# A two-layer SSD and pooling trunk step whose instruction order comes from the tile framework's other simulation

## The chip, the cores and the metric

The kernel runs on one core of one Trainium2 chip. Its metric is the device time of one execution, in microseconds (us). The text speaks of five engines: PE (matrix multiply, with PEld for its weight loads), DVE (vector), ACT (scalar, functions by table), POOL (general), and SP, which here only issues transfers.

## The reference

One inference step of a two-layer trunk with model width 1024, over one prompt of 1024 new tokens and eight samples of eight tokens each, so 1088 token columns in all. Cut to what matters:

```python
for i in range(2):
    mod = silu(c) @ ada_w[i] + ada_b[i]
    shift, scale, gate = split(mod, 3)
    hn = rmsnorm(x, norm_g[i]) * (1 + scale) + shift
    if i == 0:      # Mamba-2 SSD: in-projection, causal conv of width 4, chunked scan, gated norm, out-projection
        out, ... = ssd_branch(hn, ...)
    else:           # pooling: u, z = hn @ w_in; causal means over 2, 4, 8, 16 tokens; grouped matmul; * silu(z); @ w_out
        out, ... = pool_branch(hn, ...)
    x = x + gate * out
y = rmsnorm(x, final_norm_g)
```

The scan runs in chunks of 128 tokens over 8 groups of 4 heads. The outputs are y, the new SSM states, and the last rows of the convolution and of the pooling branch.

## The kernel before

Activations lie with the 1024 model rows on 128 partitions times 8 k blocks and the 1088 tokens along the free axis. Every fp32 operand of a large product is split in a rounded high half (`hh`, `wh`, `gh`: ACT, by L319, L139, L174, L742) and the rest as a low half (`hl`, `wl`, `gl`: DVE or POOL, by L320, L140, L176, L743), and each product is three matmuls: high by high, low by high, high by low (L182 to L184, L980 to L982, L1196 to L1198). Wide products go in two ways: plainly, in three column chunks of 364, 364 and 360 tokens, or in pairs by a scheme of seven half-size products instead of eight (`st` tiles, sums of operands in `t`).

In time the stages are these, in us from the start of the span:

- 0 to 75, the front: adaLN vectors (`am`, L253), the first norm, then for each k block the modulation (L316, L322, L323) and at once its matmuls;
- 75 to 350: the first layer's in-projections (`front_pairs`);
- 350 to 925: the scan, group by group. One step of a scan chunk is: transposes `tr` (L545, L549); from them `cb` and `xd` (DVE L559, L562) and `Bt` (ACT L566); masks `M` (ACT L556, L557); decays `cd` (ACT L574) and `ea` (ACT L543), which need `acb`, a row fetched by a transfer through a ring of two buffers; the state product `S` (PE L588); state updates (L596, L597); and `y` (PE L609, L613). Between the steps stand, as filling, further in-projections (their results leave PSUM by ACT L419) and out-projections (`mm`, whose results are gated and added by DVE L764);
- 925 to 1075: the end of the out-projection, the second layer's norm and its plain products `pl`. Here three column chunks are normalised in turn: squares summed over k (`ss`, L781), their sum over partitions (`ms`, PE L293, two matmuls), `rst` (ACT L296, L309), the scaled rows (DVE L316), shift and rounding (ACT L318, L319), and `hl` (DVE L320);
- 1075 to 1360: the fast pairs of the second layer, 1360 to 1470 the pooling and its grouped product;
- 1470 to 1632: the last out-projection, in seven blocks, the last of which is followed quarter by quarter by the final norm: `ms` (L293), `rst` (L296), the scale (L1648, L309), `y` (DVE L1661, POOL L1659) and ten transfers of the result.

The order of the instructions on each engine is not the order of the code. The tile framework's scheduler takes, for each engine, the earliest instruction of the program that its simulation says can run now. The code sets limits to it: buffer counts of the pools (two `acb`, two `wh` and `wl`, three `mm`), `issue_after`, which holds a group of instructions back behind a given one, and `keep_in_program_order`. On the chip each engine then takes its instructions strictly in the order so fixed, and waits where an operand is late.

## Time and profile before

| what | value |
| --- | --- |
| median of 3 runs | 1631.87 us |
| lowest and highest | 1627.06 and 1631.94 us |
| profiled execution, span | 1632.2 us |
| PE busy | 1601.1 us (98%) |
| DVE busy | 1290.3 us (79%) |
| ACT busy | 816.7 us (50%) |
| POOL busy | 495.2 us (30%) |
| mean granted clock of PE | 0.994 |

The profiled execution lies 0.3 us above the median of the runs. The chain of work that ended last runs over PE for 82% of the span, over DVE for 7% and over transfers for 5%. A row of a timeline gives start, busy time, engine, line, operation, tiles and shapes, and in brackets the idle time of the engine before it and what ended that.

### The profile page before, as it was taken

The page shows a single profiled execution, that of the slowest core. Times are in us where ns is not written, and L with a number is a line of the kernel's source. Part 1 is how long each engine was busy: PE and PEld are TensorE (multiplying, and loading weights), DVE is VectorE, ACT ScalarE, POOL GpSimd, SP SyncE. Part 2 cuts the span into 40 slices and gives each one's busy share as a digit, 9 for nine tenths or more (in the row PEclk, how much of TensorE's full clock was granted, in tenths as well). Part 3 has the DMA queues.
Part 4 walks back from the last instruction along what each step waited for, and adds up shares of the span by engine and source line. Part 5 has one row for each costly group of instructions (what it writes and reads, how often), then busy time and mean ns, then how long its engine had stood idle before and what let it go on. Part 6 is the DMA issues. An engine that isn't in the chain of part 4 may idle for free.

```text
span 1632.2 us, 30956 instructions
## 1 busy us (share of the span) xinstructions
PE 1601.1 (98%) x12061; PEld 1524.7 (93%) x12061; DVE 1290.3 (79%) x2140; ACT 816.7 (50%) x1565; POOL 495.2 (30%) x527
## 2 busy tenths in 40 slices
PE   8999999999999999999999999999999999999997
PEld 6899999998899888988998899999999999999997
DVE  6875779777788888789887867988889867577876
ACT  6653334456776767575645536632322333333364
POOL 0233556511221202121212222366667640000241
PEclk9999999999999999999999999999999999999999
DMA  9422232264555554668898533043333369565783
GB/s 346 163 98 84 93 109 71 105 203 133 183 162 167 165 186 135 217 232 299 276 332 284 201 137 111 29 142 112 102 112 99 129 213 367 166 170 173 167 164 119
DMA packets 122306, 275.60 MB, mean 169 GB/s; under 512 B 18192, under 2 KB 59312, under 8 KB 122160
## 3 DMA queue, kind: packets, MB, share of 16 engines
q1 hardware_dynamic: 118128, 260.91, 46.8%
q0 software_dynamic: 4032, 12.72, 4.5%
q8 instruction: 95, 1.56, 0.4%
q14 instruction: 51, 0.42, 0.1%
HBM read 201.12 MB, written 70.23 MB: 166 GB/s over the span
## 4 chain that ended last, share of the span: by engine, by line
PE 82%; DVE 7%; DMA 5%; issue 3%; ACT 2%; POOL 1%; SPq 0%; DVEq 0%; ACTq 0%; POOLq 0%
PE st L982 11%; PE st L980 11%; PE st L981 11%; PE mm L182 10%; PE mm L184 10%; PE mm L183 10%; DMA acb<-acd 2%; PE op L1197 2%; PE op L1198 2%; PE op L1196 2%; PE y L609 2%; PE S L588 2%; PE y L613 2%; PE am L253 1%; PE tr L549 1%
## 5 line engine op out<-in xcount | busy, mean ns | idle before, releaser
L982 PE MATMUL st<-hh,w 128*128 128x272 f32 x832 | 240.8, 289 | 2.3 <-DVE w L176 2.3
L980 PE MATMUL st<-hh,w 128*128 128x272 f32 x832 | 240.2, 289 | 0.0
L981 PE MATMUL st<-hl,w 128*128 128x272 f32 x832 | 239.7, 288 | 0.0
L982 PE MATMUL st<-t,w 128*128 128x272 f32 x624 | 179.6, 288 | 0.0
L980 PE MATMUL st<-t,w 128*128 128x272 f32 x624 | 179.6, 288 | 0.0
L981 PE MATMUL st<-t,w 128*128 128x272 f32 x624 | 179.2, 287 | 0.0
L182 PE MATMUL mm<-hh,wh 128*128 128x364 f32 (+1 forms) x528 | 178.4, 338 | 0.1
L184 PE MATMUL mm<-hh,wl 128*128 128x364 f32 (+1 forms) x528 | 174.6, 331 | 0.0
L183 PE MATMUL mm<-hl,wh 128*128 128x364 f32 (+1 forms) x528 | 173.7, 329 | 0.0
L174 ACT ACTIVATE w<-wr 128x512 fp32r<-128x512 f32 x104 | 65.6, 631 | 190.4 <-PE st L982 156.8
L982 PEld LDWEIGHTS st<-hh,w 128*128 128x128 f32 x832 | 156.4, 188 | 3.4 <-DVE w L176 3.4
L980 PEld LDWEIGHTS st<-hh,w 128*128 128x128 f32 x832 | 156.7, 188 | 0.3 <-issue 0.3
L981 PEld LDWEIGHTS st<-hl,w 128*128 128x128 f32 x832 | 156.8, 188 | 0.0
L596 POOL TENSOR_TENSOR hd<-h,cd 128x256 f32<-128x256 f32 x56 | 47.1, 842 | 353.6 <-DVE h L597 195.4
L182 PE MATMUL mm<-gh,wh 128*128 128x364 f32 (+1 forms) x384 | 130.2, 340 | 2.1 <-ACT raw L419 2.1
L1197 PE MATMUL op<-b,w 128*128 128x272 f32 x448 | 129.0, 288 | 1.3 <-DVE b L1126 1.3
L1198 PE MATMUL op<-b,w 128*128 128x272 f32 x448 | 129.0, 288 | 0.7 <-DVE w L1170 0.7
L1196 PE MATMUL op<-b,w 128*128 128x272 f32 x448 | 129.6, 289 | 0.0
L184 PE MATMUL mm<-gh,wl 128*128 128x364 f32 (+1 forms) x384 | 127.1, 331 | 0.0
L183 PE MATMUL mm<-gl,wh 128*128 128x364 f32 (+1 forms) x384 | 126.7, 330 | 0.1
L980 PEld LDWEIGHTS st<-t,w 128*128 128x128 f32 x624 | 117.7, 189 | 0.0
L982 PEld LDWEIGHTS st<-t,w 128*128 128x128 f32 x624 | 117.3, 188 | 0.0
(293 smaller groups left out, 4613.7 us busy)
## 6 DMA issues: line engine op xcount, KB each, us to landing
wr<-win SPq DMA_DIRECT2D x48, 512.0 KB, 3.7
acb<-acd SPq DMA_DIRECT2D x64, 256.0 KB, 3.9
wr<-pin SPq DMA_DIRECT2D x32, 512.0 KB, 3.6
wr<-pout SPq DMA_DIRECT2D x28, 512.0 KB, 3.9
x<-x1d SPq DMA_DIRECT2D x24, 544.0 KB, 6.3
x1d<-x SPq DMA_DIRECT2D x22, 544.0 KB, 5.4
wr<-pout POOLq DMA_DIRECT2D x20, 512.0 KB, 5.5
x<-xT SPq DMA_DIRECT2D x16, 544.0 KB, 6.0
```

The costliest lines, as they stand in the source:

```text
L174: self.nc.scalar.activation(hi, src, AF.Copy)
L182: nc.tensor.matmul(ps[:, :n], hi[:, k, :], ah[:, a:a + n], start=first, stop=False)
L183: nc.tensor.matmul(ps[:, :n], hi[:, k, :], al[:, a:a + n], start=False, stop=False)
L184: nc.tensor.matmul(ps[:, :n], lo[:, k, :], ah[:, a:a + n], start=False, stop=last)
L588: nc.tensor.matmul(S[:, 256 * i:256 * i + 256], Bt, xde.rearrange("p r q -> p (r q)"), start=True, stop=True)
L596: nc.gpsimd.tensor_tensor(out=hd, in0=h[-1], in1=cd.unsqueeze(2).to_broadcast([P, 4, 64]), op=ALU.mult)
L980: nc.tensor.matmul(ps[c][:, :QUART], hi[:, k], xh[:, t], start=(k == 0), stop=False)
L981: nc.tensor.matmul(ps[c][:, :QUART], hi[:, k], xl[:, t], start=False, stop=False)
L982: nc.tensor.matmul(ps[c][:, :QUART], lo[:, k], xh[:, t], start=False, stop=(k == 3))
L1196: nc.tensor.matmul(ps[:, :QUART], hi[:, k], xh, start=k == 0, stop=False)
L1197: nc.tensor.matmul(ps[:, :QUART], hi[:, k], xl, start=False, stop=False)
L1198: nc.tensor.matmul(ps[:, :QUART], lo[:, k], xh, start=False, stop=k == 7)
```

## The change

One argument is added where the framework's context is made. The scheduler itself stays; the simulation that tells it what can run when is another, a time-line simulation in place of the default one.

```diff
-    with tile.TileContext(nc) as tc:
+    with tile.TileContext(nc, schedule_with_timeline_sim=True) as tc:
```

The instructions are the same, but for two more loads of ACT's function table, where an exponential (L484) now stands between two gate chunks. What changes is the order on each engine: on PE instructions move by up to 99 places, on DVE by up to 39, on ACT by up to 29. In the long runs of `st` matmuls (about 160 to 320 and 1080 to 1360 us) PE's order is unchanged. Three places, first ACT in the scan near 902 us. `Bt_10578` is needed by the second `S` of a step, `cd_10696` needs the transfer into `acb_10612`:

```order
+L139 ACTIVATE wh_10538<-wr_10317 128x1024
+L557 ACTIVATE M_10621<-M_10621 128x512
 L543 ACTIVATE ea_10614<-acb_10558 128x512
-L566 ACTIVATE Bt_10498<-tr_10482 128x128
-L557 ACTIVATE M_10567<-M_10567 128x512
-L556 ACTIVATE M_10621<-acb_10558,tka_1431 128x128 x2
-L139 ACTIVATE wh_10538<-wr_10317 128x1024
-L556 ACTIVATE M_10621<-acb_10558,tka_1431 128x128 x2
+L566 ACTIVATE Bt_10578<-tr_10562 128x128
 L574 ACTIVATE cd_10696<-acb_10612 128x4
-L557 ACTIVATE M_10621<-M_10621 128x512
-L566 ACTIVATE Bt_10578<-tr_10562 128x128
```

`Bt_10578` moves from behind `cd_10696` to ahead of it. Next DVE at the start of the second layer, near 1000 us, in the first column chunk. `hl_11576`, `hl_11578` and so on are the low halves of the eight k blocks, `wl_11825` a weight's low half. Before:

```order
L316 TENSOR_SCALAR x_10311<-x_10311,scl_270,rst_11192 128x364
L316 TENSOR_SCALAR x_10439<-x_10439,scl_270,rst_11192 128x364
L316 TENSOR_SCALAR x_10536<-x_10536,scl_270,rst_11192 128x364
L320 TENSOR_TENSOR hl_11576<-x_10307,hh_11575 128x364
L320 TENSOR_TENSOR hl_11578<-x_10309,hh_11577 128x364
L316 TENSOR_SCALAR x_10699<-x_10699,scl_270,rst_11192 128x364
L320 TENSOR_TENSOR hl_11580<-x_10311,hh_11579 128x364
L320 TENSOR_TENSOR hl_11582<-x_10439,hh_11581 128x364
```

and now:

```order
L316 TENSOR_SCALAR x_10699<-x_10699,scl_270,rst_11192 128x364
L316 TENSOR_SCALAR x_10904<-x_10904,scl_270,rst_11192 128x364
L316 TENSOR_SCALAR x_10975<-x_10975,scl_270,rst_11192 128x364
L769 TENSOR_TENSOR x_10904<-x_10904,gs_11714 128x64
L764 TENSOR_SCALAR x_10975<-mm_11721,gat_271,x_10975 128x296
L767 TENSOR_TENSOR gs_11735<-mm_11721,gat_271 128x64
L140 TENSOR_TENSOR wl_11825<-wr_11822,wh_11824 128x1024
L320 TENSOR_TENSOR hl_11576<-x_10307,hh_11575 128x364
L769 TENSOR_TENSOR x_10975<-x_10975,gs_11735 128x64
L320 TENSOR_TENSOR hl_11578<-x_10309,hh_11577 128x364
L320 TENSOR_TENSOR hl_11580<-x_10311,hh_11579 128x364
L316 TENSOR_SCALAR x_10307<-x_10307,scl_270,rst_11192 128x364
```

All eight L316 of the chunk, the end of the out-projection and the weight's split now stand ahead of the first `hl`, and the next chunk's eight L316 ahead of the fourth. On PE the first chunk's `ms` moves there from ahead of the last matmul of one product to behind the eighth of the second product after it, 20 matmuls on. Last PE near 1614 us, in the last block, where `ms_18611` and `ms_18658` are the sums for the first two quarters of the final norm:

```order
 L1197 MATMUL op_18631<-b_18406,w_18361 128x272
 L1198 MATMUL op_18631<-b_18406,w_18362 128x272
+L1196 MATMUL op_18678<-b_18248,w_18367 128x272
+L293 MATMUL ms_18611<-ss_18142,ones 128x272
 L293 MATMUL ms_18658<-ss_18142,ones 128x272
-L1196 MATMUL op_18678<-b_18248,w_18367 128x272
 L1197 MATMUL op_18678<-b_18248,w_18367 128x272
```

`ms_18611` moves one product (24 matmuls) back, to beside `ms_18658`; in the same way the third quarter's `ms_18705` moves to beside `ms_18751`, behind the last product.

## Prediction

> **What bounds the kernel now.** I read the page first, then the list of what PE waits for, then windows and timelines around those waits.
>
> ```profile
> span 1632.2 us, 30956 instructions
> PE 1601.1 (98%) x12061; PEld 1524.7 (93%) x12061; DVE 1290.3 (79%) x2140; ACT 816.7 (50%) x1565; POOL 495.2 (30%) x527
> ```
>
> PE is busy for 1601.1 of 1632.2 us. The change leaves every matmul in place, so it can act only on the 31.1 us in which PE stands, and on the clock. PE's waits, the columns being total, count and longest:
>
> ```profile
> PE S L588 <- ACT Bt L566: 4.5, 3, 2.3
> PE pl L182 <- ACT hh L319: 2.6, 2, 1.9
> PE st L982 <- DVE w L176: 2.3, 5, 0.6
> PE mm L182 <- ACT hh L322: 2.3, 2, 1.8
> PE mm L183 <- DVE hl L323: 2.1, 2, 1.8
> PE mm L182 <- ACT raw L419: 2.1, 1, 2.1
> PE y L613 <- DVE h L593: 1.4, 1, 1.4
> PE op L1198 <- DVE w L1170: 0.7, 1, 0.7
> ```
>
> These are 18.0 us; the last matmuls are followed by a tail of outputs. So there is little to win, and any engine that reaches PE's operands later loses directly. In the two long runs of st products PE's order is the same before and after. What can move lies in the front, the scan, the start of layer 1 and the tail. A wait can cost more than its length. Windows, columns length, busy time of PE, PEld, DVE, ACT, POOL, then granted clock, DMA share, GB/s:
>
> ```profile
> 733.00:737.00 4.00, 4.00 (x18) 3.92 (x17) 3.38 (x4) 4.00 (x7) 2.23 (x2) 0.57 0.26 103
> 904.00:908.00 4.00, 4.00 (x38) 3.53 (x35) 4.00 (x7) 1.87 (x6) 1.54 (x2) 0.57 0.97 254
> 1025.00:1030.00 5.00, 4.75 (x27) 4.38 (x28) 4.79 (x17) 5.00 (x17) 1.93 (x5) 1.00 0.00 0
> ```
>
> The first window follows the 2.1 us wait for raw, the second the 2.3 us wait for Bt, the third a 1.95 us wait for hh. At 0.57 over 4 us the clock was halved for about 3.4 us (4 x 0.43 / 0.5), a loss of some 1.7 us of work each; after 1.95 us it stayed whole. The Trainium skill ("TensorE: Matmul & The Clock Gate", section "HAM oscillation — how this bites in real kernels") gives as its abstract rule no idle gaps over about 3.4 us; the trace shows half clock after shorter ones, so the measurement decides.
>
> **The change part by part.** The matmuls and their operands stay; two loads of ACT's function table come in, between gate chunks near 90 us. The loads in the timelines last 1.28 us; st products there need ACT only for weights (L174), and PE has waited for none of those, so I cost them at nothing; uncovered they would be 2.6 us.
>
> *Scan, 890 to 925 us: -5.0.* PE's three waits for Bt come from ACT's order: cd (L574) needs the next acb transfer and stands ahead of Bt (L566).
>
> ```profile
> 902.23 0.21 ACT L574 ACTIVATE cd<-acb 128x4 f32<-128x4 f32 x1 [1.56 <-DMA acb<-acd]
> 902.88 0.28 ACT L566 ACTIVATE Bt<-tr 128x128 f32<-128x128 f32 x1
> ```
>
> In the new order this Bt stands ahead of that cd, and PE puts a first S, then 24 matmuls of two output products, then the second S. The 4.5 us and the 1.7 us of half clock can both go: -6.2. The transfer is then late only for cd, which POOL needs a step later. The end of the good side is -6.2, of the bad side -2.0 (only the 2.3 us wait goes and 0.3 comes back); I take -5.0, near the full sum, because two of the three places have Bt moved so.
>
> *Start of layer 1, 998 to 1042 us: +6.5.* Here three column chunks are normalised in turn: ms (PE L293), rst (ACT L296, L309), eight scalings (DVE L316), eight shifts and roundings (ACT L318, L319), eight low halves (DVE L320), then the plain products pl.
>
> ```profile
> 997.24 0.88 PE L293 MATMUL ms<-ss,ones 128*128 128x364 f32 x2
> 998.76 0.51 ACT L309 ACTIVATE rst<-rst 128x364 f32<-128x364 f32 x1
> 999.30 2.63 DVE L316 SCALAR_TENSOR_TENSOR x<-x,scl,rst 128x364 f32<-128x364 f32 x5 [0.38 <-ACT rst L309]
> 1001.85 0.98 DVE L320 TENSOR_TENSOR hl<-x,hh 128x364 fp32r<-128x364 f32 x2
> 1004.06 0.33 PE L182 MATMUL pl<-hh,wh 128*128 128x364 f32 x1
> 1007.07 1.04 ACT L139 ACTIVATE wh<-wr 128x1024 fp32r<-128x1024 f32 x1
> 1010.48 1.22 DVE L140 TENSOR_TENSOR wl<-wr,wh 128x1024 fp32r<-128x1024 f32 x1
> 1025.22 0.43 PE L182 MATMUL pl<-hh,wh 128*128 128x360 f32 x1 [1.95 <-ACT hh L319]
> ```
>
> Before, the first low half is ready at 1002.4, ahead of the first pl at 1004.06. Now the first ms stands 20 matmuls later (about 20 x 0.166 us), so rst is there at about 1002.9 rather than 999.3. DVE then does all eight L316 (8 x 0.51 = 4.1), three small steps (0.7) and wl (L140, 1.1) before the first hl: 1002.9 + 5.9 + 0.5 = 1009.3. On ACT wh (L139) now stands behind one L318: hh comes at about 1006.0. PE, free at about 1004.8 (the second ms stands ahead of pl), waits until 1006.0, runs two matmuls and waits until 1009.3: 1.2 + 2.9. Three of eight k groups later it needs the fourth hl, which stands behind the eight L316 of the second chunk (rst about 1010.2, ready 1010.3 + 4.1 + 0.9 = 1015.3): another 3.0. So the first chunk's products end 7 us late. Then some comes back: the second chunk's operands are all there, and its 48 matmuls hide the third chunk's chain, so the 0.6 and 1.95 us waits of before go, and 23 matmuls of the next pair now fill the third chunk's start. Against that stand 0.8 us for the third chunk's narrow low halves (L333, now behind L904), and 1.0 us for the next weights (L139 again). By this count the sum is +4.8; waits of 2.9 and 3.0 us lie above the 2.3 that halved the clock, so I add one 1.7: +6.5. Bounds: +2 (hh and hl overlap better than counted) and +10.
>
> *Tail, 1611 to 1632 us: +2.5.* The log of the first quarter's sum, and with it the final scaling, hang on ms L293, which now stands a product later, beside the second; the third stands beside the fourth, behind the last product.
>
> ```profile
> 1614.00 0.40 ACT L1648 ACTIVATE ms<-rst 128x272 f32<-128x272 f32 x1
> 1614.44 2.13 DVE L1661 SCALAR_TENSOR_TENSOR y<-x,vec,ms 128x272 f32<-128x272 f32 x5 [2.73 <-ACT ms L1648]
> 1616.49 11.76 SPq L1662 DMA_DIRECT2D yT<-y  x10
> 1618.00:1620.00 2.00, 2.00 (x17) 1.92 (x16) 1.91 (x6) 1.37 (x4) 1.39 (x2) 1.00 1.00 341
> 1624.00:1628.00 4.00, 0.00 (x0) 0.00 (x0) 2.54 (x6) 1.16 (x3) 1.48 (x2) 0.98 1.04 347
> 1624.80 2.54 DVE L1661 SCALAR_TENSOR_TENSOR y<-x,vec,ms 128x272 f32<-128x272 f32 x6 [2.33 <-ACT ms L1648]
> ```
>
> Once started, the output transfers hold all DMA engines (share 1.00 to 1.04) to the end, so a later start ends later. One product is 24 matmuls, about 3.3 us; the table load, now done while ACT waits, gives 1.0 back: the first y comes at about 1616.7 instead of 1614.44, +2.3. The other way of counting agrees: the third quarter's six y (2.54) now follow the last product, where only the fourth's six did. +2.5, between +1.9 and +3.0.
>
> *Scan, 725 to 775 us: 0.* Before, ACT's gh (L742) waits for gr and holds up L419, which frees PE's accumulator.
>
> ```profile
> 729.80 1.11 ACT L742 ACTIVATE gh<-gr 128x1088 fp32r<-128x1088 f32 x1 [0.88 <-DMA gr<-gyd]
> 731.50 0.45 ACT L419 ACTIVATE raw<-mm 128x364 f32<-128x364 f32 x1
> 740.00:745.00 5.00, 5.00 (x34) 4.59 (x33) 4.86 (x9) 4.72 (x6) 0.00 (x0) 1.00 0.96 323
> ```
>
> Now L419 stands ahead of this gh, and PE does tr and S of two scan steps first: the 2.1 us and its 1.7 us of half clock can go, -3.8. But scan steps then follow each other with fewer matmuls between, and DVE (4.86 of 5.00) has the same work. Adding ACT's and DVE's rows in the new order, I find PE waiting 0.3 for xs, 1.5 for z (L702) and 1.6 for an accumulator that L764 clears late: 3.4 in place of 3.8. I take 0, between -3.8 and +4.0 (twice those waits).
>
> *Front, 20 to 75 us: -1.5.* The order of the k blocks' steps changes: weight splits (L140) are pulled ahead, so that none stands right ahead of a late block's low half (L323).
>
> ```profile
> 55.00:75.00 20.00, 18.18 (x132) 14.71 (x132) 19.91 (x30) 11.84 (x20) 10.29 (x5) 1.00 0.22 69
> 62.67 1.21 DVE L140 TENSOR_TENSOR wl<-wr,wh 128x1024 fp32r<-128x1024 f32 x1
> ```
>
> DVE is full (19.91 of 20), so what is moved ahead of one block is late for another; that L140 (1.2) lies right before the hl PE waits 1.8 for. I take -1.5, between -3.0 and +1.5.
>
> *Three small places: +2.5.* A weight split near 140 us is needed 9 us earlier (PE's waits for L176 were up to 0.6, for L1170 0.7, for h L593 1.4). With such a wait more at 140 (1.0), 405 (0.8) and 1590 us (0.7) it is +2.5, between 0 and +5.
>
> The sum: -5.0 + 6.5 + 2.5 + 0 - 1.5 + 2.5 = +5.0 on the profiled 1632.2, that is 1637.2. The median of the runs, 1631.87, lies 0.3 below the profiled span: 1636.9.
>
> **The rivals.** About 0.3% (4.9 us) is what a measurement of this kernel can tell from no change: below 1627.0 is faster, above 1636.8 slower.
>
> *Faster: the start of layer 1 costs nothing.* If ms is accumulated earlier than I count, DVE's eight L316 fall under matmuls and the +6.5 goes; the scan then also gives its full -6.2 and -3.8: 5.0 - 6.5 - 1.2 - 3.8 = -6.5, about 1625.4. It decides where the first hl comes before 1005 us. For it: the waits removed are real and were followed by half clock. Against: eight L316 and an L140 between rst and hl are in the order, and their rows last 5.2 us.
>
> *Much slower: scan steps too dense.* If the packed steps at 725 to 775 cost 4.0 and the second wait at layer 1 halves the clock once more (1.7), the time is 1636.9 + 5.7 = 1642.6. For it: DVE's 4.86 of 5.00 there. Against: ACT had idle time to give.
>
> *The new waits cost only their length.* As after the 1.95 us wait, where the clock stayed 1.00, the clock might stay whole at layer 1: 1636.9 - 1.7 = 1635.2. By the skill's rule on gaps quoted above this is what would happen, since none of the new waits reaches 3.4 us.
>
> **How the numbers follow.** My forecast holds 0.52, spread over about 1632 to 1642, half of it above 1636.8; faster 0.16; much slower 0.17; the clock whole 0.15, nearly all within 0.3%. So slower 0.26 + 0.17 + 0.02 = 0.45, same 0.26 + 0.12 = 0.38, faster 0.16 + 0.01 = 0.17. The bounds of the terms reach from -12 to +23 together but not at once; 1627 leaves out most of the faster rival, 1647 is the dense case with half of the other upper bounds; the forecast's own range is 1632 to 1642.
>
> **What would show it.** In the new profile: S waits for Bt down from 4.5 to under 1.5 us and clock 1.00 at 900 to 910; pl waiting for hl L320 and hh L319 for about 7 us, in two or three pieces, near 1005 to 1015; first y (L1661) about 2.3 us later against the last matmul, DMA share 1.0 after it; no 2.1 us wait for raw L419, and shorter ones for L702 or L764 instead. I am wrong if pl waits for less than 3 us, or if new waits of several us stand at places I cost at nothing, the pool mixing stage at 1360 to 1470 us first, whose loads are reordered on SP.

## The result and the profile after

The changed kernel takes 1654.14 us (median; 1651.64 to 1655.32) against 1630.42 us for the kernel before, measured beside it: a ratio of 1.014, 95% interval 1.0125 to 1.0154. The forecast was 1636.9 us with a range of 1627 to 1647. The sign was right; the time lies 17 us above the forecast and 7 us outside the range. The profiled execution has a span of 1649.9 us, 17.7 more than before. The medians lie further apart, 23.7 us: the profiled execution is the fastest of the four of the changed kernel, and that of before is a slow one (three later profiles of the same kernel, the probes below, reach the end of PE's products 1.1, 3.9 and 5.6 us earlier). What follows accounts for the 17.7.

The head of the page and the list of what PE waits for, after the change:

```profile
span 1649.9 us, 30991 instructions
PE 1615.4 (98%) x12061; PEld 1521.4 (92%) x12061; DVE 1291.6 (78%) x2140; ACT 812.7 (49%) x1567; POOL 516.3 (31%) x527
```

```profile
PE pl L183 <- DVE hl L320: 3.9, 2, 2.7
PE mm L182 <- ACT hh L322: 3.3, 4, 1.0
PE ms L293 <- DVE rst L1315: 2.0, 1, 2.0
PE S L663 <- ACT xs L660: 1.9, 2, 1.1
...
PE mm L182 <- DVE gin L1096: 1.3, 1, 1.3
PE pl L182 <- ACT hh L319: 1.3, 1, 1.3
```

PE does not wait much more than before: 34.5 us of the span (1649.9 - 1615.4) against 31.1. Its busy time has grown by 14.3 us, for the same 12061 matmul records. The prediction had excluded just that. Where it grew is seen when the same stretch of PE's work is cut out of both traces: the scan with the products in it, 4246 records in each. The columns are length, then busy time of PE, PEld, DVE, ACT and POOL, then clock, DMA share and GB/s. Before:

```profile
384.00:941.00 557.00, 550.40 (x4246) 499.65 (x4246) 461.16 (x764) 352.43 (x802) 103.37 (x157) 0.99 0.64 215
```

and after:

```profile
382.00:948.00 566.00, 563.90 (x4246) 494.99 (x4245) 457.05 (x761) 348.95 (x801) 113.83 (x158) 1.00 0.63 210
```

In this stretch PE waits for 2.1 us instead of 6.6, the clock is better, and PE is busy for 13.5 us longer. The difference does not come in jumps, as a wait's would. If the k-th matmul in PE's queue is taken in both traces and its start compared, the lag of the new kernel is -2.5 us at 384 us, +1.4 at 508, +3.8 at 641, +6.4 at 745, +8.8 at 811 and +10.5 at 877 (time in the kernel before).

One row of matmuls shows what has changed. This is the timeline of PE for a `y` of the scan before (each fp32 matmul leaves two records, so these 32 are 16 matmuls):

```profile
544.12 0.44 PE L609 MATMUL y<-M,xd 128*64 128x128 f32 x4
544.39 0.39 PE L613 MATMUL y<-ea,h 128*64 128x128 f32 x4
...
545.70 0.39 PE L613 MATMUL y<-ea,h 128*64 128x128 f32 x4
546.02 0.43 PE L182 MATMUL mm<-hh,wh 128*128 128x364 f32 x1
546.29 0.33 PE L183 MATMUL mm<-hl,wh 128*128 128x364 f32 x1
```

its weight loads:

```profile
544.12 0.20 PEld L609 LDWEIGHTS y<-M,xd 128*64 128x64 f32 x4 [0.17 <-issue]
...
546.02 0.19 PEld L182 LDWEIGHTS mm<-hh,wh 128*128 128x128 f32 x1 [0.17 <-issue]
```

and the same `y` after, first on PE, then on its weight loads:

```profile
550.42 0.44 PE L609 MATMUL y<-M,xd 128*64 128x128 f32 x4
...
551.13 0.39 PE L613 MATMUL y<-ea,h 128*64 128x128 f32 x4
551.45 0.43 PE L184 MATMUL mm<-hh,wl 128*128 128x364 f32 x1
551.72 0.38 PE L545 MATMUL tr<-xbc,xbc 128*128 128x128 f32 x2
551.94 0.49 PE L549 MATMUL tr<-kc,xbc 128*128 128x128 f32 x3
552.36 0.66 PE L609 MATMUL y<-M,xd 128*64 128x128 f32 x8
552.95 0.43 PE L182 MATMUL mm<-hh,wh 128*128 128x364 f32 x1
...
559.49 0.66 PE L613 MATMUL y<-ea,h 128*64 128x128 f32 x8
```

```profile
550.01 0.19 PEld L183 LDWEIGHTS mm<-hl,wh 128*128 128x128 f32 x1
550.42 0.20 PEld L609 LDWEIGHTS y<-M,xd 128*64 128x64 f32 x4 [0.22 <-DVE xd L562]
...
551.45 0.19 PEld L184 LDWEIGHTS mm<-hh,wl 128*128 128x128 f32 x1 [0.17 <-issue]
551.55 0.35 PEld L545 LDWEIGHTS tr<-xbc,xbc 128*128 128x128 f32 x2
...
552.36 0.42 PEld L609 LDWEIGHTS y<-M,xd 128*64 128x64 f32 x8 [0.17 <-issue]
```

Before, the 16 matmuls stood in one run. After, they come in three pieces, with products, transposes and an `am` between. Where a product follows `y`, it takes 0.27 us to the next matmul (546.02 to 546.29, 551.45 to 551.72, and 552.95 to 553.22 in the same timeline) where products follow each other at 0.17. This interval alone is no measure of a loss: behind transposes it is 0.25 us too (555.94 to 556.19 in the same timeline), and the probes below find no loss there. The weight loads tell more. Where `y`, whose weight tile is 64 columns wide, meets a tile of 128 columns, PEld stands for about 0.17 us (`issue`: nothing the profile shows holds it) instead of loading under the matmul before: once ahead of the run and once behind it before the change, and at both ends of each piece after it (0.17 to 0.41 us). The Trainium skill ("TensorE: Matmul & The Clock Gate", section "Architectural detail: the array is 16× 32×32, not 1× 128×128") says that PE's queue can take weight loads ahead of running matmuls. From product to product the trace agrees, with a median gap on PEld of 0.00 us over the 2000 steps of the scan after; at the 68 changes from a tile 64 columns wide to a product the median gap is 0.17 us, and the measurement decides.

So the theory to be tested was that a change on PE between two sorts of matmul has a price. Which sort was open for long: any change of kind (`mm`, `y`, `tr`, `S` and so on; theory A in what follows), a change between fp32r and fp32 (theory B, the first that was held; fp32r is the type of the rounded halves, in which the large products run), or a change of the weight tile's width (theory C, the last). The rival was that PE loses in the scan through waits on other engines.

### The profile page after: what moved, and what is told of

Read it like the earlier page. It is cut to its first block, busy times and chain, and to the rows that moved or that the text cites. A ratio compares the mean times of both kernels' runs of the same rounds, so it can differ in the third digit from the quotient of the medians.

```text
span 1649.9 us, 30991 instructions
## 1 busy us (share of the span) xinstructions
PE 1615.4 (98%) x12061; PEld 1521.4 (92%) x12061; DVE 1291.6 (78%) x2140; ACT 812.7 (49%) x1567; POOL 516.3 (31%) x527
## 5 line engine op out<-in xcount | busy, mean ns | idle before, releaser
L1196 PE MATMUL op<-b,w 128*128 128x272 f32 x448 | 127.3, 288 | 2.9 <-ACT b L1125 1.7
L1197 PE MATMUL op<-b,w 128*128 128x272 f32 x448 | 127.9, 288 | 0.0
L1198 PE MATMUL op<-b,w 128*128 128x272 f32 x448 | 127.3, 288 | 0.0
```

The lines of the kernel that those rows point to most:

```text
L1196: nc.tensor.matmul(ps[:, :QUART], hi[:, k], xh, start=k == 0, stop=False)
L1197: nc.tensor.matmul(ps[:, :QUART], hi[:, k], xl, start=False, stop=False)
L1198: nc.tensor.matmul(ps[:, :QUART], lo[:, k], xh, start=False, stop=k == 7)
```

## The experiments

All but the probes keep the program's instructions and fix the order of queueing, as the first diff shows. Their time is compared with the kernel before, run beside them. For the scan they are compared by a *net time*: the time from PE's 2651st to its 5951st matmul (384 to 941 us before), less PE's idle time there, less half of the time at half clock. This is worked out from each trace. In the five traces that have the order of before in this stretch unchanged (the kernel before, the layer-1 run and the probes) it is 546.4 to 547.1 us, while the waits in it differ by up to 3 us.

### PE's order alone, and the other engines' alone

```diff
         Build(tc, io).run()
+        _pin(tc, PINS)   # PE alone: each instruction queued behind the one listed ahead of it
```

The first is the new kernel with PE in the order of before, the second the kernel before with PE in the new order. In both the scheduler orders the other engines anew around it.

> The changed kernel (time-line simulation), with PE's instructions queued in the order of the kernel before; the other engines' orders are the scheduler's own. Switching (every change of PE between fp32r products and fp32 matmuls such as tr, S, y costs about 0.1 us, and the new order has some 140 more of them in the scan): PE busy falls from 1615 back to about 1601, time 1630 to 1640. Late operands (the new orders of ACT and DVE feed PE late, in waits too short to be listed): time stays above 1648 with PE busy near 1615.

> The kernel before (default simulation), with PE's instructions queued in the changed kernel's order; the other engines' orders are the scheduler's own. Switching: PE busy about 1615 and time 1645 to 1660, since PE's order alone carries the cost. Late operands: PE busy near 1601 and time 1630 to 1640.

Measured: 1702.84 us (ratio 1.0447, 1.0428 to 1.0465) and 1679.76 us (1.0309, 1.0282 to 1.0336). Both are slower than either kernel; in the first, PE waits long for the states `h`:

```profile
PE y L613 <- DVE h L593: 19.3, 5, 4.4
PE y L613 <- DVE h L597: 8.5, 5, 2.1
```

The times alone do not decide between the two expectations, since new waits cover what PE's order does. The net time of the scan does: 546.4 us with PE in the order of before and 561.5 with PE in the new order, whatever stands on the other engines; the kernels themselves have 546.7 and 562.6. The 15.9 us are in PE's own order.

### A stretch of the new order at a time

```diff
+        _pin(tc, PINS)   # all five engines: order of before, but the new order from A to B us
```

A to B is 384 to 885 us in the first; 78 to 384 and 885 to 932 in the second; 990 to 1066 in the third.

> The kernel before, all five engines queued in its own order, but in the scan from 384 to 885 us in the changed kernel's. Switching: the 13 us that PE's instructions lag behind in that stretch of the changed kernel come back here, 1641 to 1646, PE busy up by 10 to 14, with few new waits. Late operands only of other stages: 1628 to 1634.

> The kernel before, all five engines queued in its own order, but from 78 to 384 us and from 885 to 932 us in the changed kernel's, where the changed kernel gained (waits for st weights, for the state update at 371 and for Bt). If the gains stand alone: 5 + 4.4 us less, 1619 to 1624, faster than both kernels. If they were only the other side of a loss elsewhere (work put off): 1628 to 1634.

> The kernel before, all five engines queued in its own order, but from 990 to 1066 us, the start of the second layer, in the changed kernel's. The prediction's term (first hl behind eight L316): 5 to 7 us more, 1635 to 1637, with pl waiting for hl L320 about 4 us. If that loss hangs on the scan that precedes it: within 2 us of the kernel before.

Measured: 1645.09 us (1.0108, 1.0077 to 1.014), net scan 559.5; 1627.21 us (0.9989, 0.9978 to 1.0001); 1634.47 us (1.0025, 1.0012 to 1.0038). The scan's new order alone is enough to lose most of what the kernel loses. The start of layer 1 loses some 4 us (2.0 to 6.2; 5 to 7 were expected), by the very waits that the new kernel shows there, with 0.9 more for `hl` (L333) and 0.5 for `wh` (L139):

```profile
PE pl L183 <- DVE hl L320: 3.9, 2, 2.7
PE pl L182 <- ACT hh L319: 1.3, 1, 1.3
```

The second run gained less than expected: at the seam near 384 us a `tr` waited 2.3 us for Bt, with half clock behind it, and took back some 4 of the 5.3 us gained up to there.

### Fewer or more changes on PE

First, products of one accumulator brought together in the new order, so that changes between fp32r and fp32 in the scan fall from 344 to 222: with the other engines scheduled anew, and with them fixed.

```diff
-mm mm mm | y y | mm | tr tr tr tr | y y y y | mm ...
+mm mm mm mm ... | y y | tr tr tr tr | y y y y
```

> The changed kernel, with PE's order changed in the scan alone: the matmuls of one product are brought together again where scan matmuls stood between them, so that PE changes between the kinds 222 times there instead of 344 (202 in the kernel before). Switching: 122 x 0.11 = 13 us less, 1637 to 1646. Late operands or slower transfers: 1650 or more, as the same work is done with scan matmuls later.

> The changed kernel with every engine queued in its own order, but PE's matmuls of one product in the scan brought together, 222 changes of kind instead of 344, the other engines left as they are. Switching: 122 changes fewer give 8 to 13 us back, less what scan steps that come later then make PE wait, 1640 to 1648. Without a cost of switching: 1654 or more.

Measured: 1667.14 us (1.0227, 1.0207 to 1.0246) and 1664.92 us (1.0223, 1.0197 to 1.025). Both miss the time expected. Steps of the scan came later, and PE waited for that (`gl` L743 alone 8.7 us in the first); but the net time of the scan also fell only from 562.6 to 556.5 and 559.1, where 122 fewer changes of type should have given nearly all of the 15.9 us. The changes between fp32r and fp32 are not what costs.

Next, pieces of `y`, `tr` or `S` joined to the next piece of their kind, in the new order:

```diff
-y y | mm mm mm | tr tr tr tr | y y
+mm mm mm | tr tr tr tr | y y y y
```

> The new order on all engines, but 46 times in the scan a piece of y, tr or S that stands alone is moved to right ahead of the next piece of the same kind (past at most 20 matmuls). Changes between kinds of product on PE (mm, y, tr, S, am, xs) in the scan fall from 498 to 430, y's pieces from 94 to 61; changes between fp32r products and fp32 ones from 344 to 304. Theory A (every change of kind costs about 0.096 us, 15.9 us over 162 more changes): -6.5 against the new order, about 1647.5. Theory B (only a change between fp32r and fp32 costs, 0.112 us): -4.5, about 1649.5. Rival (the scan's loss is waits of PE on the other engines): no gain, 1654 or more.

Measured: 1654.89 us (1.0139, 1.012 to 1.0158), no gain. Net of waits the scan fell by 7.3 us to 555.4, a little more than theory A asks; but pieces held back were late for others. In the scan PE now waits for 9.4 us in place of 2.1:

```profile
PE y L644 <- DVE zsc L631: 4.4, 2, 2.5
```

Then the other way: three cuts into the order of before, each adding changes of one sort.

```diff
-y y y y y y y y | mm mm mm mm mm mm ...
+y y y y | mm mm mm mm mm mm | y y y y ...      (24 places)
```

```diff
-tr tr tr tr | y y ...
+tr tr | y y | tr tr | ...                      (24 places)
```

```diff
-S S | tr tr tr tr
+S | tr tr | S | tr tr                          (16 places)
```

> The order of before on all engines, but 24 times in the scan a run of y matmuls is cut in half and six product matmuls (fp32r) put between the halves. 48 more changes of kind, and 48 more changes between fp32r and fp32. Theory A: 48 x 0.096 = +4.6 us. Theory B: 48 x 0.112 = +5.4. Rival (waits): within 1 us of before, since every y ends at most 1 us later.

> The order of before on all engines, but 24 times in the scan two of the next y matmuls are put between the transposes tr of a step. 48 more changes of kind, none of them between fp32r and fp32 (both are fp32). Theory A: +4.6 us. Theory B: 0. Rival (waits): within 1 us of before.

> The order of before on all engines, but 16 times in the scan two of the next step's transposes tr are put between the two S matmuls of a step. 32 more changes of kind, none between fp32r and fp32, none of the width of the weight tile (all 128 columns). Theory A (0.096 us per change of kind): +3.0 us. Theory B (fp32r against fp32): 0. Theory C (0.157 us per change of width): 0.

Measured, with the changes counted in PE's queue over the scan:

| scan | changes of kind | fp32r to fp32 and back | changes of width | net scan, us | time, ratio |
| --- | --- | --- | --- | --- | --- |
| before | 336 | 202 | 161 | 546.7 | |
| `y` cut by products | 384 | 250 | 209 | 553.7 | 1.0032 (1.0021 to 1.0043) |
| `tr` cut by `y` | 384 | 202 | 193 | 551.9 | 1.0039 (1.0024 to 1.0053) |
| `S` cut by `tr` | 368 | 202 | 161 | 546.8 | 0.999 (0.9973 to 1.0007) |
| products together, fixed | 416 | 222 | 231 | 559.1 | 1.0223 (1.0197 to 1.025) |
| pieces joined | 430 | 304 | 197 | 555.4 | 1.0139 (1.012 to 1.0158) |
| after | 498 | 344 | 257 | 562.6 | 1.014 (1.0125 to 1.0154) |

The second cut adds no change between fp32r and fp32 and costs 5.2 us: theory B falls. The third adds 32 changes of kind and costs nothing: theory A falls. The changes of width, between weight tiles of 128, 64 and 32 columns, go with all rows. Over the fifteen scans of this document (the two kernels and all runs but the layer-1 one and the probes) a straight line through the net times gives 0.153 us per change of width, and misses by 1.0 us on average (root mean square), 2.4 at most. Lines through the changes of type or of kind instead miss by 3.4 and 1.6. From before to after that is 96 changes, or 14.7 of the 15.9 us; 77 of the 96 lie at `y` (91 to 168).

### The price by itself

The kernel before, followed by matmuls on PE alone: 48 of one sort and 48 of another, in runs of 48 down to runs of 1.

```diff
+for run in (48, 12, 3, 1):      # later probes: (48, 1)
+    for b in range(0, 48, run):
+        for i in range(run): one(b + i)
+        for i in range(run): two(b + i)
```

> The kernel before, with PE alone at the end: 48 fp32r matmuls (128x364) and 48 fp32 ones, in runs of 48, 12, 3 and 1, once with the fp32 shape of y (64x128) and once with that of S (128x256). Nothing else runs there. Switching: the stretch in runs of 1 is about 95 x 0.1 = 9 us longer than that in runs of 48, for both shapes, and in proportion between. If the scan's matmuls were slowed by other engines or transfers, all four stretches last the same.

> PE alone after the kernel's work, six pairs of matmul kinds, 48 of each, in runs of 48 and then in runs of 1. Theory C (width of the weight tile): runs of 1 take about 0.22 us more per change for the pairs fp32r 128 wide with fp32 64 wide (128 columns moving), fp32r 128 with fp32r 64, fp32 128 with fp32 64, and nothing more for fp32r 128 with fp32 128 and for fp32r 128 with fp32r 128. Theory B (type): more for the pairs fp32r with fp32 whatever the width, nothing for the pairs of one type. The pair fp32r 128 with fp32 64 of 256 columns moving shows whether a longer matmul hides the change.

> PE alone after the kernel's work, five pairs of matmul kinds, 48 of each, in runs of 48 and then in runs of 1: fp32r 128 wide with fp32 64 wide in the lower column half; the same in the upper half; fp32r 128 with fp32r 64 in the lower half; fp32 128 with fp32 64 in the lower half; fp32 64 lower with fp32 64 upper. If the width decides for fp32 whatever the place, pairs 1, 2 and 4 take about 0.22 us more per change in runs of 1 (21 us each), pair 5 nothing, and only fp32r is free. If the place decides, pair 2 alone is dear, and pairs 1, 3 and 4 are free.

In the first, fp32r 128x364 products with fp32 tiles 64 wide and 128 columns moving took 13.6 us in runs of 48, 14.6 in runs of 12, 20.5 in runs of 3 and 34.8 in runs of 1, that is 0.22 us per change; with fp32 tiles 128 wide and 256 moving 28.6, 28.7, 28.6 and 28.5, where 9 us more had been expected of both. In the second probe, windows in pairs (runs of 48, then of 1): fp32r 128 with fp32 64 wide; fp32r 128 with fp32 128 wide; fp32r 128 with fp32r 64 wide; fp32 128 with fp32 64 wide.

```profile
1634.66:1648.59 13.93, 13.93 (x146) 13.53 (x144) 0.00 (x0) 0.00 (x0) 0.00 (x0) 1.00 0.01 2
1648.59:1683.44 34.85, 34.85 (x147) 18.10 (x145) 0.00 (x0) 0.00 (x0) 0.00 (x0) 1.00 0.00 0
1683.45:1702.19 18.74, 18.74 (x146) 18.74 (x145) 0.00 (x0) 0.00 (x0) 0.00 (x0) 1.00 0.00 1
1702.19:1720.75 18.56, 18.56 (x147) 18.56 (x146) 0.00 (x0) 0.00 (x0) 0.00 (x0) 1.00 0.00 1
1720.75:1734.27 13.52, 13.52 (x99) 13.49 (x99) 0.00 (x0) 0.00 (x0) 0.00 (x0) 1.00 0.00 1
1734.27:1747.79 13.52, 13.52 (x99) 12.04 (x98) 0.00 (x0) 0.00 (x0) 0.00 (x0) 1.00 0.00 0
1775.30:1791.50 16.20, 16.20 (x194) 15.91 (x193) 0.00 (x0) 0.00 (x0) 0.00 (x0) 1.00 0.01 1
1791.50:1828.98 37.48, 37.48 (x195) 23.44 (x193) 0.00 (x0) 0.00 (x0) 0.00 (x0) 1.00 0.00 1
```

Runs of 1 take 0.22 us more per change of width (34.85 - 13.93 over 95 changes) with the type changing, and the same with fp32 on both sides (37.48 - 16.20). The change of type at one width costs nothing. So far theory C; but fp32r with fp32r is free even where the width changes (13.52 and 13.52), and theory C had said otherwise. PEld shows the dear case (the first two rows) and a free one (the last two):

```profile
1669.98 0.19 PEld L1798 LDWEIGHTS pF<-pf 128*64 128x64 f32 x2 [0.18 <-issue]
1670.34 0.19 PEld L1798 LDWEIGHTS pR<-pr 128*128 128x128 f32 x1 [0.17 <-issue]
...
1739.87 0.13 PEld L1798 LDWEIGHTS pF<-pr 128*64 128x64 f32 x1
1740.03 0.19 PEld L1798 LDWEIGHTS pR<-pr 128*128 128x128 f32 x1
```

The third probe puts the narrow fp32 tile in one half of the columns: in runs of 1 it takes 34.88 us in the lower half and 34.88 in the upper, against 34.85 above, so the place does not matter. In runs of 48 one half alone takes 18.95 and 18.81 us instead of 13.93, so per change the difference is 0.17 there and not the 0.22 expected, and it is the same 0.17 with fp32 on both sides (21.49 and 37.39 us). The fifth pair, narrow fp32 tiles in the lower and the upper half, says why: in runs of 48 each takes 0.22 us, in runs of 1, with the halves in turn, 0.11. Two neighbours in different halves thus share their time, and the long runs of the first two probes, which alternate the halves, had that gain, while a narrow tile between wide ones has no such neighbour. Of the 0.22 us, 0.05 is this lost gain, and 0.17 the change itself. The pieces of `y` in the scan keep their pairs of halves, and 0.153 is near 0.17. Fp32r with narrow fp32r in the lower half, 128 columns moving, takes 10.98 and 13.35 us, 0.025 per change. What is dear is a change of width with an fp32 tile on the narrow side. Why fp32r escapes was not found, and tiles 32 columns wide were not probed.

### The order of before with fewer changes

```diff
+        _pin(tc, PINS)   # before; new order 78-350 us (and 885-932 in the first and third);
+                         # 16, 11 and 12 pieces of y, tr or S joined to the next
```

> The order of before, with the new order of all engines from 78 to 350 us and from 885 to 932 us, and 16 pieces of y, tr or S in the scan joined to the next piece of their kind (changes of kind 354 to 335). From the runs before: -3.6 for the st products, -3.5 for the S waits, -2.3 if the wait near 735 us goes again, -1.8 for the changes by theory A (0 to -0.4 by theory B): about 1619 to 1623, faster than both kernels.

> The order of before, with the new order of all engines from 78 to 350 us, and 11 pieces of y, tr or S in the scan joined to the next piece of their kind past product matmuls only (changes of width 161 to 141). -3.6 for the st products, by theory C 20 x 0.157 = -3.1 for the scan: about 1624 to 1626 if no new wait comes of it.

> As the run before it, with the new order of all engines from 885 to 932 us too (waits of S for Bt), and changes of width 155 in all. -3.6, -3.5 for the S waits, by theory C 6 x 0.157 = -0.9: about 1622 to 1625.

Measured: 1629.32 us (0.9992, 0.9982 to 1.0002), 1634.26 us (1.0016, 1.0 to 1.0031) and 1632.22 us (1.0002, 0.9987 to 1.0017), against the 1619 to 1626 expected. The net scan stayed within 1 us of the line (545.9, 544.8 and 547.2 us for 149, 141 and 155 changes of width), but the pieces held back delay the steps after them. In the second:

```profile
PE tr L545 <- ACT Bt L566: 7.3, 5, 1.6
PE S L588 <- ACT Bt L566: 5.6, 6, 2.7
```

These are 12.9 us of waits for Bt where the kernel before has 4.5. None of the versions tried is faster than the kernel before by more than the measurement can tell; all three are faster than the changed one.

## Why the prediction was wrong, step by step

The step that failed is the first: "The change leaves every matmul in place, so it can act only on the 31.1 us in which PE stands, and on the clock." Every matmul is there, but what a matmul takes depends on its neighbour in the queue. The prediction compared PE's order at places with waits; it did not count over the whole scan how often `y`, `am` and the like now break into other work (161 to 257 changes of width), and so put this term at nothing. At 0.153 us each the missing term is +14.7, and the sum of +5.0 would have become +19.7, against 17.7 between the two profiles and 23.7 between the medians. The trace of before already showed such changes, by PEld's 0.17 us at 544.12 and 546.02, though not their price. All the signs that the prediction named for its being wrong were waits; the loss came as busy time of PE.

Two sums of the text do not come out as written. The bounds of its terms add up to -9.1 and +21.5, not to -12 and +23. And the terms shown for layer 1 give 7.1 - 2.55 + 1.8 = 6.35, not 4.8; the 1.5 between must stand for the 23 matmuls that fill the third chunk's start, to which no figure is given.

The lag of PE's k-th matmul gives the other terms. It compares two single executions, and where waits differ from execution to execution, the other traces with the order of before say how much of it is the change's:

- *Scan, 890 to 925 us, -5.0:* the waits of `S` for Bt are gone, the granted clock from 908 to 916 us of the new profile is 1.00, and from 877 to 941 us the lag falls by 3.4 us with the dearer matmuls in it. Right that the waits go; the size stays open, since the traced kernel before was slow just here. Four other traces with its order in this stretch are 2.5 to 4.4 us faster over it too, and `S` waits 2.0 to 4.7 us for Bt in them.
- *Start of layer 1, +6.5:* +5.3. Right in mechanism and place: `hh` 1.26, `hl` 2.74 and 1.20 us against 1.2, 2.9 and 3.0 counted, and the half clock behind the second wait came. But the 1.7 us of half clock lie ahead of the third wait, whose end DVE sets: PE came later and waited that much less (1.20 + 1.7 = 2.9). By these rows the 1.7, counted on top of the 3.0, cost nothing more.

```profile
1015.13 0.43 PE L182 MATMUL pl<-hh,wh 128*128 128x364 f32 x1 [1.26 <-ACT hh L319]
1018.47 0.43 PE L183 MATMUL pl<-hl,wh 128*128 128x364 f32 x1 [2.74 <-DVE hl L320]
1024.46 0.43 PE L183 MATMUL pl<-hl,wh 128*128 128x364 f32 x1 [1.20 <-DVE hl L320]
```

```profile
1018.00:1023.00 5.00, 4.53 (x18) 4.50 (x18) 5.00 (x12) 5.00 (x13) 0.00 (x0) 0.66 0.52 143
```

- *Tail, +2.5:* +1.9. The first `y` of the final norm starts 4.48 us ahead of PE's last product in place of 6.79 (1621.23 before): 2.31 later, as counted.

```profile
1632.01 4.17 DVE L1661 SCALAR_TENSOR_TENSOR y<-x,vec,ms 128x272 f32<-128x272 f32 x10 [1.59 <-ACT ms L1648]
1636.49 0.29 PE L1198 MATMUL op<-b,w 128*128 128x272 f32 x1
```

- *Scan, 725 to 775 us, 0:* PE's wait for raw (2.1 us) is gone, and two waits for xs (L660), 1.9 us, stand in its place, again with half clock behind them (0.66 over 738 to 743 us). Right as a sum, though not by the waits named: 0.3 was counted for xs, 1.5 for z and 1.6 for an accumulator.
- *Front, -1.5:* +2.2, the wrong sign in this pair of traces. `ms` waits 2.0 us for rst (L1315) instead of 0.7, and four short waits for hh (3.3) replace two (2.3); the gain for hl (2.1 to 0.7) was there. Some of it is chance: with the order of before that wait for rst is 0.2 to 2.0 us, and one such trace has a lag of 1.2 us here.
- *Three small places, +2.5:* near 140 us nothing came; from 78 to 357 us the five waits of st for w (2.3 us) went instead, and the lag fell by 3.8. At 1356 us a wait for gin (1.3) came, at a stage that the text had named as one to watch. In sum about -2, so the forecast of +2.5 had the wrong sign.
- *A place costed at nothing:* from 941 to 1001 us the lag rose by 1.5 us, with PE's waits for gh (L742, 1.0) and gl (L743, 0.8) of the out-projection.

The rival "scan steps too dense" had the right sign and a part of the right place, but by waits for DVE, and 4 us; in the new scan PE waits less than before. The rival "the new waits cost only their length" is out, by the half clock behind the 2.74 us wait. But the limit that the prediction read from its windows (half clock after 2.1 us, whole after 1.95) is none: the same wait of `pl` for `hh`, 1.95 to 2.04 us long in twelve traces of this document, has half clock behind it in eight and whole clock in four.

## What to carry to other kernels

Before reordering a bound engine, count in the new queue not only waits but neighbours: another simulation in the same scheduler broke runs of like matmuls into pieces, and no list of waits showed it. On PE, keep fp32 matmuls with narrow weight tiles in unbroken runs; here each break into 128-wide work cost about 0.15 us on either side. Joining them afterwards must not hold back what the next steps need: in the new order three attempts won 3.5 to 7.3 us of net time and lost it, or more, in new waits.

## What was not expected of the hardware

With PE alone, a change between fp32 tiles 64 wide and tiles 128 wide costs 0.17 us, and the weight load is then not taken under the matmul before; alternating with wide tiles also loses the time that two narrow tiles in different column halves share, 0.05 us per change. A longer moving operand does not hide it: with 256 columns moving, 48 pairs took 44.8 us in runs of 1 and 18.7 in runs of 48, 0.27 us per change. By estimate 0.11 of that is the lost sharing (half of 0.22 us, the time of such a tile in the long run), which leaves 0.16 or 0.17 again. A change between fp32r and fp32 at one width costs nothing (18.74 and 18.56 us), nor does one between fp32r tiles of 128 and 64 columns with 256 moving.
